# Two stacked transformer blocks on one core: the tile scheduler orders the instructions by a full timeline of the engines

## The chip, the cores and the metric

The kernel runs on one core of a Trainium2 chip. The metric is the device time of one execution in microseconds (us), the median over three runs. The engines are TensorE (PE, with PEld for its weight loads), VectorE (DVE), ScalarE (ACT), GpSimd (POOL) and SyncE (SP); each works through its own instructions strictly in the order in which they stand in its program, and waits on semaphores for the others.

## The reference

256 tokens of width 1024 go through two blocks of two layers each, all in float32:

```python
# first block, i = 0, 1
h = h + (ab_mixer if i == 0 else nsa_mixer)(rms_norm(h, g), ...)   # retention + mLSTM, or sparse attention
h = h + conv_ffn(rms_norm(h, ffn_norm_g[i]), ...)                  # 1024 -> 2 x 2816 -> 1024
e = rms_norm(p[i] @ ple_w[i], ple_norm_g[i])
h = h + sigmoid(rms_norm(h, ple_gate_norm_g[i]) @ ple_w_gate[i]) * e
# second block, l = 0, 1: hybrid layer
h = rms_norm_2(x, norm_g) * (1 + scale) + shift
a_qkv, a_z, m_cq, m_ckv, m_kr, m_z, merge = split(h @ w_in)
y_a = dilated_mixer(a_qkv, rel_bias) * silu(a_z)      # 24 heads in 3 groups, bias by distance, softmax
y_m = mla_mixer(m_cq, m_ckv, m_kr, ...) * silu(m_z)   # 16 heads, low-rank q and kv, causal softmax
merged = g_a * (y_a @ w_out_a) + g_m * (y_m @ w_out_b)
x = x + gate * (merged @ w_o)
# at the end rms_norm_2(x, final_norm_g)
```

## The kernel before

The 256 tokens are two blocks of 128 rows (tb0 and tb1). The activations stay in SBUF; what streams is weights, 253 MB of DMA, in tiles of 128 x 1024. Each weight tile takes three steps in `wt()`: SP issues the DMA into `raw` (L442, five buffers), ACT rounds it to `whi` (L448), and DVE subtracts to get the rest, `wlo` (L449); both have four buffers. PE then computes every product three times in float32r (`mm3`, L465 to L467):

```python
mm(out, lhsT=a[0], rhs=b[0], start=start, stop=False)
mm(out, lhsT=a[0], rhs=b[1], start=False, stop=False)
mm(out, lhsT=a[1], rhs=b[0], start=False, stop=stop)
```

Activations are split likewise after a transpose on PE (L577), into `xh` by ACT (L581) and `xl` by DVE (L582). Products gather in `acc` tiles, of which PSUM holds three.

The phases run one after the other: the AB mixer (0 to 130 us), FFN, PLE gate (341 to 372), the sparse attention NSA (372 to 530), FFN, PLE gate (723 to 753), the two hybrid layers (753 to 1110 and 1110 to 1480) and the last norm. Within a phase the program is written as one list of operations; the order on each engine is the choice of the tile scheduler, which takes the operations whose inputs and buffers it expects to be there.

In the AB mixer retention and mLSTM attend in pieces (scores L812, L813 and L828, DVE weights L816 and L818, outputs L820 to L822). Their heads are then squared on ACT (L855), reduced on DVE (L856), and an inverse root is found by integer and Newton steps on DVE (L591 to L595). `cat` (L873 for retention, L895 for mLSTM) takes that and the gates, and its transposes (L577) feed the output product. PLE computes one norm on POOL (L627 to L631, `half` L960), and its update of `h` (L966) needs it.

In a hybrid layer `quad` attends with four heads at a time. For each head a bias tile is fetched by a DMA on the ACT queue into one of two buffers; the scores come from PE (L1466), DVE adds the bias and finds the maximum (L1469), ACT takes the exponent (L1474), DVE normalises (L1475, L1476), PE transposes (L677), DVE and ACT copy (`pT`, L680, L682) and PE multiplies by v (`po`, L685, L688). `mla_chunk` does the same for the other attention (scores L1557, exponent L1562):

```python
bt = ph.tile([P, 1024], F32, tag="bias", bufs=2, name=self.nm("bias"))
nc.scalar.dma_start(bt, bass.AP(b0.tensor, ...))
nc.vector.tensor_tensor_reduce(p[:, g0:g1], s3, b3[:, g0:g1, T - nk:], -1.0, 3e38, ALU.add,
                               ALU.min, nm[:, j:j + 1])
```

Products of `w_in` that follow in the program are what the scheduler can put between the steps of these chains.

Of the kernel before, what the change touches and what calls it, by code (L numbers as in the profile page):

```python
# [16 lines left out]
T = 256  # L17
# [4 lines left out]
W = 1024  # L22


# ------------------------------------------------------------------ layout
# The weights are cut into tiles of at most 128 x 1024 in the order in which
# the kernel consumes them.  A tile is a list of pieces (array, index, rows,
# columns) laid side by side.
# [28 lines left out]
def plan():  # L57
# [6 lines left out]
    def nat(key, arr, ix, cols, nkb, row0=0):  # L64
        """tiles of row blocks x 512 columns"""
        per = W // len(cols)
        for t in range(0, nkb, per):
            add((key, t // per), [(arr, ix, row0 + kb * P, cols) for kb in range(t, min(nkb, t + per))])

    def tr(key, arr, ix, cols, nkb=8):  # L70
        """one tile per 128 columns, all row blocks"""
        add((key, 0), [(arr, ix, kb * P, cols) for kb in range(nkb)])

    # AB mixer
# [31 lines left out]
    # NSA mixer  # L106
# [15 lines left out]
    # hybrid layers  # L122
# [70 lines left out]
# per-feature vectors as columns of one [128, n] array  # L193
# [72 lines left out]
def pack_rows(inp):  # L266
    """vectors that are spread over all partitions by the load"""
    return np.concatenate([inp["ple_norm_g"][0], inp["ple_norm_g"][1], inp["final_norm_g_2"],
                           inp["b_ada_2"][0][2048:], inp["b_ada_2"][1][2048:], inp["c_2"][0]])[None, :]


def constants():
    """[128, n] tables that depend on shapes alone"""
# [4 lines left out]
    # rotary tables of the retention, [2 heads x 64, 256]  # L278
# [7 lines left out]
    # swap of the halves of each head  # L286
# [4 lines left out]
    # decay of the retention in [key, query]: 256 queries for key block 0, 128 for block 1  # L291
# [10 lines left out]
    # NSA: causal mask of the last key block, validity of the compressed keys  # L302
# [13 lines left out]
    # sum of four partial sums that lie below each other  # L316
    c["nsa.st4"] = (p[:, None] % 32 == np.arange(30)[None, :]).astype(f)
    c["nsa.blk"] = (p[:, None] // 16 == np.arange(8)[None, :]).astype(f)
    # rotary tables of the MLA, rows: even heads, odd heads, cos, sin; columns: frequency, quarter
    # turns, phase, amplitude  # L320
# [21 lines left out]
    # buckets of the relative positions, reversed: column m is the distance 255 - m  # L342
# [30 lines left out]
# ------------------------------------------------------------------ kernel  # L373
class Builder:
# [54 lines left out]
    # -- weights: load, split into two float32r parts  # L429
    def wt(self, key, dst=None):  # L430
        """dst: pairs of tiles for the two parts, one for each block of rows or one for all"""
# [4 lines left out]
        if dst is None:  # L436
            # in the FFN some go where the PLE keeps its weights
# [24 lines left out]
    def mm3(self, out, a, b, start, stop):  # L462
        """out += a^T b with a = (hi, lo), b = (hi, lo)"""
# [5 lines left out]
    def gates(self, key, n, xs):  # L469
        """x W for n columns: [128 tokens, 2, n] in PSUM"""  # L470
# [11 lines left out]
    def nat(self, key, xs, nkb, w=512, fill=False, last=0, sc=False):  # L482
        """x W for both blocks of 128 tokens: two [128, w] in PSUM.  last: the first block is done early"""
# [26 lines left out]
    def nat_tb(self, key, xs, dst, evac, early):  # L510
        """x W for 1024 columns: the first block of tokens is done before the second, by all products of that
        if early, else by those of the last 512 columns.
        dst(c, t): where the parts of the weights go, evac(columns, tb, acc)"""
# [30 lines left out]
    def tr(self, keys, xs, nkb=8, w=P):  # L544
        """(x W)^T for one or two blocks of columns: [w, 2, 256] in PSUM"""
# [7 lines left out]
    def tr_start(self, keys, xs):  # L553
        """as tr, blocks in banks of their own, the first half of the rows of all blocks before the second:
        it can begin when half of x is there"""
# [10 lines left out]
    def make_xT(self, src, nkb, gain=None, dst=None):  # L566
        """src(tb, kb): [128 tokens, 128 features].  Transposed, times gain, split."""
# [18 lines left out]
    # -- 1/sqrt of a small tile, by Newton steps from an estimate in the exponent  # L586
# [15 lines left out]
    def meansq(self, dst, src):  # L602
        """a column of the sums of src^2 / 2048"""
# [3 lines left out]
    def rstd(self, src, name):  # L607
        """1/rms of the rows of src [128, 2, 1024]: [128, 2]"""
# [12 lines left out]
    def norm_newton(self, n, tb, j=1, eng=None):  # L621
        """Newton steps from an estimate in the exponent, for one block of tokens; the sum is in columns 0 and j"""
# [3 lines left out]
        # x is half the mean; the sign of y turns with each of the three steps  # L626
# [6 lines left out]
    def norm_tb(self, tb):  # L633
        """the norm of h for one block of tokens, at the end of the part before the one that needs it"""
# [15 lines left out]
    def row_bc(self, col, name):  # L650
        """[128, 2] per token -> [128, 256], the same row in all partitions"""
# [15 lines left out]
    def pv_pair(self, po, p0, p1, v, ns, start):  # L667
        """po [2 heads x 64, 256 queries] += v^T p^T over ns sources.  p0(e, s): [128 queries, 128 keys] of
        the first query block, p1(e, s): [128, 256] of the second, v(s, kb, e): [128 keys, 64]"""
# [39 lines left out]
    # ---------------------------------------------------------------- AB mixer  # L709
    def ab(self):  # L710
# [9 lines left out]
        # input and forget gates, [token, 4 + 4]  # L720
# [4 lines left out]
        # q, k of the mLSTM: convolution over time, silu (times 2)  # L725
# [17 lines left out]
        # v with a column of ones  # L743
# [9 lines left out]
        # log sigmoid(x) = min(x, 0) - 2 atanh((1 - t) / (3 + t)), t = tanh(|x| / 2)  # L753
# [13 lines left out]
        # rows over the tokens: i, log f  # L767
# [21 lines left out]
        # q, k of the retention: rotary  # L789
# [60 lines left out]
        # norms over each head  # L850
# [26 lines left out]
        # den = max(|den|, exp(-m)); 0.5 / den * rsqrt(ss / (128 den^2) + eps)  # L877
# [22 lines left out]
    # ---------------------------------------------------------------- FFN  # L900
# [33 lines left out]
    # ---------------------------------------------------------------- PLE  # L934
    def ple(self, i):
# [5 lines left out]
        # e = rms(p W) g / 2  # L941
# [34 lines left out]
    # ---------------------------------------------------------------- NSA mixer  # L976
    def nsa(self):
# [9 lines left out]
        # keys and values of the two branches  # L987
        def head_factor(src, nh, out, scale):
            """r * rsqrt(r^2 ss / 64 + eps) * scale for each head of src(tb) [128, nh, 64]: out [128, 2, nh]"""
# [12 lines left out]
        # raw keys and values of the compression, [2 tokens x 64, group, 256]  # L1002
# [39 lines left out]
        # in the places of tensors that are not there yet  # L1042
# [5 lines left out]
        # gates  # L1048
# [11 lines left out]
        def compress(kv):  # L1060
            n = "kv"[kv]
            # four row blocks at once, side by side in the array
# [10 lines left out]
            # gelu, tanh form  # L1073
# [66 lines left out]
        def attention(g, qT):  # L1140
            # compressed branch, all heads of the group at once
# [66 lines left out]
    # ---------------------------------------------------------------- tables of the hybrid layers  # L1208
    def rope_tables(self):
        """[128, 4, 256]: q of the even heads, q of the odd heads, cos, sin"""  # L1210
# [34 lines left out]
    def bias_rows(self):  # L1245
        """biases by distance, invalid distances at -1e30, in DRAM: 23 copies of
        [8 heads, 3 groups, 384], so that the row of
        partition 16 a + b, 16 a + b places earlier, can be read from copy a + b with positive strides"""
# [23 lines left out]
    def side_work(self):  # L1272
        """work that waits for nothing, done beside products that leave VectorE idle"""
# [7 lines left out]
    def ada(self):  # L1281
        """shift and scale as columns [128, 16], the gate in all partitions [128, 1024]"""
# [9 lines left out]
        # silu(c) along the rows  # L1292
# [34 lines left out]
    # ---------------------------------------------------------------- hybrid layer  # L1327
# [390 lines left out]
```

## Time and profile before

| | before |
|---|---|
| median of three runs (lowest, highest) | 1482.52 us (1481.35, 1489.27) |
| span of the profiled execution | 1490.1 us |
| PE busy / PEld busy | 1431.5 us (96%) / 1220.8 us (82%) |
| DVE busy | 1034.1 us (69%) |
| ACT busy / POOL busy | 759.8 us (51%) / 26.4 us (2%) |
| chain that ended last | PE 81%, DVE 7%, DMA 5%, ACT 3%, issue 2%, POOL 2% |

The profiled execution is one run of its own. Its span, from the first to the last instruction, lies just above the slowest of the three timed runs, 0.5% above their median; nothing around the span is recorded for it. A busy PE in these rows is a PE with a matmul in its pipe; that it goes at full pace is only seen from the rate of matmuls and from the busy share of PEld.

### The profile page before, as it was taken

What the parts mean: (1) busy time and instruction counts of PE and PEld (TensorE: products, weight loads), DVE (VectorE), ACT (ScalarE), POOL (GpSimd) and SP (SyncE); (2) the same over time, 40 slices, a digit from 0 to 9 for tenths busy, and PEclk for the clock granted to TensorE, in tenths of its full rate; (3) what the DMA queues carried; (4) which work ended last, traced back from release to release, by engine and by line L of the source; (5) the groups of instructions that cost most, each with busy time, mean ns of one, the idle gap of its engine ahead of it and who ended that gap; (6) DMA issues with size and microseconds to landing.
All of it is one profiled execution on the core that took longest, in us unless ns stands there. A gap on an engine that the chain in (4) does not pass through costs nothing.

```text
span 1490.1 us, 23718 instructions
## 1 busy us (share of the span) xinstructions
PE 1431.5 (96%) x9011; PEld 1220.8 (82%) x9011; DVE 1034.1 (69%) x2250; ACT 759.8 (51%) x1383; POOL 26.4 (2%) x41
## 2 busy tenths in 40 slices
PE   8999979999999999999989999999999999999997
PEld 7878979988755699997787878879879797979886
DVE  7678758987777788897677744556577865456466
ACT  6355635536455665553557543434555753334443
POOL 0000000003000000000300000000000000000000
PEclk9999989999989999999999999989999999999999
DMA  7444556895630266687533444525553444443561
GB/s 264 140 146 156 177 174 232 307 322 193 235 128 1 70 214 213 213 297 280 192 127 93 147 151 128 177 70 191 188 197 129 125 147 130 142 151 117 191 200 61
DMA packets 72734, 253.99 MB, mean 170 GB/s; under 512 B 8187, under 2 KB 11795, under 8 KB 72469
## 3 DMA queue, kind: packets, MB, share of 16 engines
q1 hardware_dynamic: 68880, 239.87, 48.5%
q10 hardware_dynamic: 3740, 12.61, 2.9%
q8 instruction: 71, 1.16, 0.3%
q14 instruction: 43, 0.35, 0.1%
HBM read 251.36 MB, written 1.93 MB: 170 GB/s over the span
## 4 chain that ended last, share of the span: by engine, by line
PE 81%; DVE 7%; DMA 5%; ACT 3%; issue 2%; POOL 2%; SPq 0%; POOLq 0%; ACTq 0%; DVEq 0%
PE acc L465 21%; PE acc L467 21%; PE acc L466 21%; PE po L685 4%; PE tp L677 3%; DMA raw<-weights 3%; DVE wlo L449 2%; DMA bias<-brow 2%; PE sc L1178 2%; PE sc L1466 1%; ACT whi L448 1%; PE po L688 1%; POOL rs L631 1%; PE sc L1557 1%; DMA gb<-rows 1%
## 5 line engine op out<-in xcount | busy, mean ns | idle before, releaser
L449 DVE TENSOR_TENSOR wlo<-raw,whi 128x1024 fp32r<-128x1024 f32 (+2 forms) x386 | 460.6, 1197 | 216.8 <-ACT whi L448 213.2
L448 ACT ACTIVATE whi<-raw 128x1024 fp32r<-128x1024 f32 (+2 forms) x386 | 398.7, 1036 | 356.1 <-PE acc L467 184.6
L465 PE MATMUL acc<-xh,whi 128*128 128x256 f32 (+1 forms) x1360 | 390.1, 288 | 17.1 <-DVE zp L920 8.8
L466 PE MATMUL acc<-xl,whi 128*128 128x256 f32 (+1 forms) x1360 | 389.6, 287 | 0.7 <-DVE xl L582 0.7
L467 PE MATMUL acc<-xh,wlo 128*128 128x256 f32 (+1 forms) x1360 | 388.0, 286 | 0.5 <-DVE wlo L449 0.3
L465 PEld LDWEIGHTS acc<-xh,whi 128*128 128x128 f32 (+1 forms) x1360 | 261.0, 192 | 26.5 <-DVE zp L920 9.0
L466 PEld LDWEIGHTS acc<-xl,whi 128*128 128x128 f32 (+1 forms) x1360 | 261.4, 192 | 4.5 <-issue 2.5
L467 PEld LDWEIGHTS acc<-xh,wlo 128*128 128x128 f32 (+1 forms) x1360 | 261.2, 192 | 1.5 <-DVE wlo L449 0.9
L465 PE MATMUL acc<-whi,xh 128*128 128x512 f32 (+2 forms) x688 | 249.1, 363 | 2.3 <-DVE xh L1355 1.2
L467 PE MATMUL acc<-whi,xl 128*128 128x512 f32 (+2 forms) x688 | 248.9, 363 | 1.3 <-DVE xl L582 1.2
L466 PE MATMUL acc<-wlo,xh 128*128 128x512 f32 (+2 forms) x688 | 248.4, 361 | 0.0
L465 PEld LDWEIGHTS acc<-whi,xh 128*128 128x128 f32 x688 | 130.3, 189 | 24.0 <-ACT xh L581 2.2
L467 PEld LDWEIGHTS acc<-whi,xl 128*128 128x128 f32 x688 | 130.0, 189 | 22.2 <-DVE xl L582 2.5
L466 PEld LDWEIGHTS acc<-wlo,xh 128*128 128x128 f32 x688 | 130.3, 189 | 19.2 <-issue 1.7
L465 PE MATMUL acc<-whi,gh 128*128 128x512 f32 x176 | 70.1, 398 | 0.0
L467 PE MATMUL acc<-whi,gl 128*128 128x512 f32 x176 | 69.4, 394 | 0.0
L466 PE MATMUL acc<-wlo,gh 128*128 128x512 f32 x176 | 69.3, 394 | 0.0
L680 DVE COPY pT<-tp 128x384 f32<-128x384 f32 x56 | 31.2, 557 | 41.6 <-PE tp L677 41.4
L677 PE MATMUL tp<-const_g,pr 128*128 128x128 f32 x336 | 56.9, 299 | 0.7 <-DVE pr L1566 0.7
L677 PEld LDWEIGHTS tp<-const_g,pr 128*128 128x128 f32 x336 | 38.9, 149 | 19.4 <-issue 12.3
L682 ACT ACTIVATE pT<-tp 128x384 f32<-128x384 f32 x56 | 27.1, 485 | 45.8 <-PE tp L677 40.7
L1466 PE MATMUL sc<-qk,qk 64*128 64x256 f32 (+1 forms) x192 | 41.9, 379 | 8.6 <-DVE nmx L1469 8.1
(411 smaller groups left out, 1914.8 us busy)
## 6 DMA issues: line engine op xcount, KB each, us to landing
raw<-weights SPq DMA_DIRECT2D x384, 512.0 KB
adw<-weights SPq DMA_DIRECT2D x48, 512.0 KB
bias<-brow ACTq DMA_DIRECT2D x16, 512.0 KB
w<-weights SPq DMA_DIRECT2D x8, 512.0 KB
raw<-weights SPq DMA_DIRECT2D x8, 416.0 KB
const_ab<-consts SPq DMA_DIRECT2D x1, 1536.0 KB
h<-x SPq DMA_DIRECT2D x4, 256.0 KB
gb<-rows ACTq DMA_DIRECT2D x2, 512.0 KB
```

The lines of the kernel that those rows point to most:

```text
L448: nc.scalar.activation(hi, r, AF.Copy)
L449: nc.vector.tensor_tensor(lo, r, hi.bitcast(F32), op=ALU.subtract)
L465: mm(out, lhsT=a[0], rhs=b[0], start=start, stop=False)
L466: mm(out, lhsT=a[0], rhs=b[1], start=False, stop=False)
L467: mm(out, lhsT=a[1], rhs=b[0], start=False, stop=stop)
L631: ts(y[:, o], t[:, o], 1.5, y[:, o], ALU.subtract, ALU.mult)
L677: nc.tensor.transpose(tp[:, j * P:(j + 1) * P], a, self.ident)
L680: nc.vector.tensor_copy(pT, tp[:, :384])
L682: nc.scalar.activation(pT, tp[:, :384], AF.Copy)
L685: nc.tensor.matmul(po[e * 64:e * 64 + 64, :], lhsT=v(s, 0, e), rhs=pts[e][:, 0:T], start=start and s == 0, stop=False)
L1178: nc.tensor.matmul(s4, lhsT=qT[hs, pr, tb * P:(tb + 1) * P], rhs=kT[hs, g, :, 0:nk], start=True, stop=True)
L1466: nc.tensor.matmul(s3[:, g - g0], lhsT=qs[g][hs, pr, tb * P:(tb + 1) * P], rhs=ks[g][hs, pr, :nk], start=True, stop=True)
```

## The change

One argument of the tile context in `kernel()` is new. With it the scheduler still builds the order of each engine from the same operations, but decides which operation comes next by a timeline of all engines that it keeps while it goes, where its default goes by a simpler estimate. Comments were removed as well, without a change of the line numbers. No operation, tile, buffer count or queue is changed.

```diff
-    with tile.TileContext(nc) as tc:
+    with tile.TileContext(nc, schedule_with_timeline_sim=True) as tc:
         with ExitStack() as ctx:
             Builder(ctx, tc, aps).run()
```

The programs of the engines hold the same instructions before and after, but for one load of a function table less on ACT (the sine of L1238 now comes ahead of the first gelu of L926, where it stood between two). On PE 4426 of 8438 instructions stand elsewhere, by up to 186 places. POOL's order is the same, and SP's DMAs move by two places at most.

The first place is the quad attention of the first hybrid layer on PE (it begins at 875 us before). `acc_9462` is a product of `w_in` that nothing in the attention needs, the `sc` tiles are scores. Before:

```order
4752 L1466 MATMUL sc_9267<-qk_9008,qk_8945 128x256
4753 L1466 MATMUL sc_9271<-qk_9197,qk_9134 128x256
4754 L465 MATMUL acc_9462<-xh_7834,whi_9464 128x256
4755 L466 MATMUL acc_9462<-xl_7835,whi_9464 128x256
4756 L467 MATMUL acc_9462<-xh_7834,wlo_9465 128x256
4757 L465 MATMUL acc_9462<-xh_7834,whi_9464 128x256
4758 L1466 MATMUL sc_9279<-qk_8253,qk_8190 128x128
```

And the same scores of the change, with the last of the product's matmuls ahead of them:

```order
4776 L465 MATMUL acc_9462<-xh_7834,whi_9464 128x256
4777 L466 MATMUL acc_9462<-xl_7835,whi_9464 128x256
4778 L467 MATMUL acc_9462<-xh_7834,wlo_9465 128x256
4779 L1466 MATMUL sc_9279<-qk_8253,qk_8190 128x128
4780 L1466 MATMUL sc_9279<-qk_9008,qk_8945 128x128
4781 L1466 MATMUL sc_9279<-qk_9197,qk_9134 128x128
```

`sc_9271` stands at 4754 there: 24 matmuls of the product lie between it and `sc_9279`, where there were 4. Up to the scores `sc_9379` of the third head, whose bias tile is the first that has to wait for a buffer, there are 84 such matmuls in place of 24. The other three quads are changed alike.

The second place is DVE at the same scores (L1469 is the bias and maximum, L1476 the normalisation, L449 a weight split). Before:

```order
1447 L1469 ISA pr_9278,nmx_9264<-sc_9279,bias_9262 128x384
1448 L1469 ISA nmx_9264 128x1
1449 L1469 ISA pr_9291,nmx_9289<-sc_9292,bias_9287 128x512
1450 L1469 ISA nmx_9289 128x1
1451 L1475 RECIPROCAL l_9265<-l_9265 128x1
1452 L1469 ISA pr_9291,nmx_9289<-sc_9296,bias_9287 128x256
1453 L1469 ISA nmx_9289 128x1
1454 L1476 TENSOR_SCALAR pr_9266<-pr_9266,l_9265 128x768
```

And of the change:

```order
1428 L1476 TENSOR_SCALAR pr_9266<-pr_9266,l_9265 128x768
1429 L1469 ISA pr_9278,nmx_9264<-sc_9279,bias_9262 128x384
1430 L1469 ISA nmx_9264 128x1
1431 L449 TENSOR_TENSOR wlo_9591<-raw_9589,whi_9590 128x1024
1432 L1469 ISA pr_9291,nmx_9289<-sc_9292,bias_9287 128x512
1433 L1469 ISA nmx_9289 128x1
```

Four weight splits (`wlo_9591`, `wlo_9597`, `wlo_9654`, `wlo_9684`) now stand among the softmax steps of the first two biases, where there was none.

The third place is PE in the AB mixer, at the last pieces of retention (`tp_845` is an output, `acc_874` and `acc_875` a gate product). Before:

```order
372 L822 MATMUL tp_835<-vr,aw_833 128x128
373 L820 MATMUL tp_845<-vr,aw_843 128x128
374 L821 MATMUL tp_845<-vr,aw_843 128x128
375 L822 MATMUL tp_845<-vr,aw_843 128x128
376 L467 MATMUL acc_874<-whi_877,xl_100 128x512
377 L465 MATMUL acc_875<-whi_877,xh_99 128x512
```

And of the change, where `cat` is what the head norms produce:

```order
466 L813 MATMUL sc_840<-rqk 128x128
467 L820 MATMUL tp_845<-vr,aw_843 128x128
468 L821 MATMUL tp_845<-vr,aw_843 128x128
469 L822 MATMUL tp_845<-vr,aw_843 128x128
470 L577 MATMUL tp_1072<-const_g,cat 128x128
471 L577 MATMUL tp_1081<-const_g,cat 128x128
```

The 92 product matmuls that stood between the last L822 and the first transposes of `cat` now stand ahead of the retention pieces.

Elsewhere three things move. In both PLE gates DVE's weight splits go ahead by up to 21 places, and the second products of `ple_w` come 20 PE places later. At the end of the first hybrid layer and of the kernel the matmuls of the last three output tiles, which stood one tile after the other, are interleaved. The last DVE steps of tb0's final norm come to stand among those of tb1's.

## Rows read from the trace of the kernel before

**Rows 1.** The page: the span, the engines' busy shares, the clock, the weight splits.

```profile
span 1490.1 us, 23718 instructions
...
PE 1431.5 (96%) x9011; PEld 1220.8 (82%) x9011; DVE 1034.1 (69%) x2250; ACT 759.8 (51%) x1383; POOL 26.4 (2%) x41
...
PEclk9999989999989999999999999989999999999999
...
L449 DVE TENSOR_TENSOR wlo<-raw,whi 128x1024 fp32r<-128x1024 f32 (+2 forms) x386 | 460.6, 1197 | 216.8 <-ACT whi L448 213.2
```

**Rows 2.** Busy us by stretch: PE, PEld, DVE, ACT, POOL (count), clock, DMA share.

```profile
54.00:82.00 28.00, 27.40 (x142) 20.27 (x141) 15.13 (x31) 10.58 (x19) 0.00 (x0) 1.00 0.33 109
82.00:106.00 24.00, 23.36 (x105) 18.55 (x103) 20.96 (x52) 13.99 (x19) 0.00 (x0) 1.00 0.48 149
755.00:875.00 120.00, 116.36 (x846) 105.27 (x846) 81.37 (x225) 70.27 (x169) 0.00 (x0) 0.99 0.43 133
875.00:911.00 36.00, 33.63 (x191) 22.64 (x189) 19.32 (x54) 14.03 (x29) 0.00 (x0) 0.91 0.43 114
911.00:957.00 46.00, 46.00 (x383) 45.46 (x381) 19.52 (x18) 18.20 (x20) 0.00 (x0) 1.00 0.51 165
957.00:998.00 41.00, 39.29 (x224) 26.83 (x224) 22.19 (x58) 15.47 (x31) 0.00 (x0) 0.88 0.25 78
1155.00:1237.00 82.00, 79.79 (x598) 71.51 (x598) 57.23 (x164) 49.17 (x119) 0.00 (x0) 1.00 0.44 142
1237.00:1273.00 36.00, 33.87 (x193) 22.67 (x192) 19.33 (x54) 13.86 (x29) 0.00 (x0) 0.91 0.41 116
1318.00:1345.00 27.00, 24.62 (x143) 16.80 (x143) 16.54 (x50) 11.45 (x25) 0.00 (x0) 0.94 0.30 98
```

**Rows 3.** Chain that ended last, 868 to 900 us: start, us, what.

```profile
868.06 0.12 PE acc L467
...
879.12 0.48 ACT pr L1474
879.60 7.70 DMA bias<-brow
887.42 0.69 DVE pr L1469
```

**Rows 4.** Timeline of DVE in the AB mixer: start, us, line; idle before in brackets.

```profile
82.75 0.69 DVE L856 TENSOR_REDUCE ssr<-sqj 128x4 f32<-128x512 f32 x1 [2.37 <-ACT sqj L855]
...
87.15 0.17 DVE L595 SCALAR_TENSOR_TENSOR r<-rst,r 128x8 f32<-128x8 f32 x1
87.35 0.17 DVE L593 TENSOR_TENSOR rst<-r 128x8 f32<-128x8 f32 x1
...
90.04 0.36 DVE L863 TENSOR_SCALAR f<-r,half 128x4 f32<-128x4 f32 x2
...
95.02 1.28 DVE L873 TENSOR_TENSOR cat<-gt,f 128x512 f32<-128x512 f32 x2
...
104.77 1.28 DVE L895 TENSOR_TENSOR cat<-gt,f 128x512 f32<-128x512 f32 x2
```

**Rows 5.** Timelines of POOL and DVE in the first PLE gate.

```profile
352.79 4.78 POOL L631 TENSOR_SCALAR rs<-mt,rs 128x1 f32<-128x1 f32 x1
...
360.98 0.30 POOL L631 TENSOR_SCALAR rs<-mt,rs 128x1 f32<-128x1 f32 x1
...
352.78 4.63 DVE L449 TENSOR_TENSOR wlo<-raw,whi 128x1024 fp32r<-128x1024 f32 x4
...
363.31 0.75 DVE L966 SCALAR_TENSOR_TENSOR h<-gt,half,h 128x512 f32<-128x512 f32 x1 [3.61 <-POOL half L960]
```

**Rows 6.** Chain that ended last, from 1476 us to the end: start, us, what.

```profile
1475.83 0.23 PE acc L465
...
1484.22 0.28 DVE mt L630
...
1485.89 0.72 ACT o L1647
```

## The prediction

> **What bounds the kernel now.** I read the page first. PE is busy for 96% of the span, but PEld only for 82%, and the row of the clock has single slices below full speed [rows 1]. A share of 96% would leave 60 us to gain, if it were true. It is not the whole truth, so the next view is busy time by stretch [rows 2]. The reader should compare two kinds of stretch there. From 911 to 957 us PE has nothing but products: 383 matmuls in 46 us, PEld busy for 45.46 of 46, clock 1.00. That is the pace at which the kernel can go, one matmul in 0.12 us [rows 3]. From 875 to 911, the quad attention just ahead of it, PE is called busy for 33.63 of 36 us, but PEld only for 22.64, and the granted clock is 0.91 on average: part of the stretch runs at 1.2 GHz in place of 2.4. The other quads look the same, and the two MLA stretches look so in a milder form. So PE bounds the kernel, and what it loses lies in the attention stretches, where it works in the beat of a chain through DVE, ACT and a DMA. The chain of waits shows the heaviest link [rows 3]: the exponent of the second head at 879.12, behind it on ACT's queue the third bias, 7.70 us of DMA, and only at 887.42 the DVE step that reads it.
>
> The sum is made against the profiled execution, 1490.1 us, and carried to the median of the runs (1482.5) by their ratio, 0.995.
>
> **The change part by part.** Nothing is added or removed except one table load on ACT, so all cost and gain is in where PE stands still.
>
> *The four quads, a gain.* What is lost there in plain sight is idle time and clock; clock lost is length times (1 - clock). From [rows 2]: 875 to 911, 2.37 + 36 x 0.09 = 5.6; 957 to 998, 1.71 + 41 x 0.12 = 6.6; 1237 to 1273, 2.13 + 3.24 = 5.4; 1318 to 1345, 2.38 + 27 x 0.06 = 4.0. Together 21.6 us. Behind that lies a loss that PE's row doesn't show. Had PEld been as busy as in the product stretch (98.8%), it would have had 35.6 us instead of 22.6 in the first quad, and likewise 40.5, 35.6 and 26.7 in the others: 49.4 us of shortfall in all. That is an upper bound, because a matmul of the attention takes longer than its weight load. The new order puts 84 matmuls of products, not 24, ahead of the scores that stand behind the third bias. The 60 more are 60 x 0.12 = 7.2 us of work against a wait of about 2.3 us, so the wait is covered even if the chain itself becomes 2 or 3 us later by the products that stand in it (20 more of them ahead of the second scores, 2.4 us). Those products need four more weight splits during the softmax, 4 x 1.2 = 4.8 us on DVE [rows 1], which is busy for 19.32 of 36 there: the room exists, but the chain gets longer by part of it. I take 28 us for the four, above the plain loss because the whole stretch fills up, and far from the upper bound. Bounds: 9 (the idle time alone, no clock) to 45.
>
> *The MLA stretches, a gain.* 3.64 + 1.2 from 755 to 875 and 2.21 from 1155 to 1237 are 7.1 us [rows 2]; the products between the scores L1557 are fewer there than in the quads. I take 4, between 0 and 7.
>
> *The AB mixer, a loss.* Today 92 product matmuls, 21 us at 0.23 each [rows 6], run while DVE does the head norms; PE loses only 0.6 us from 54 to 82 and 0.64 from 82 to 106 [rows 2]. In the change these products run first, and the last retention output is followed by nothing but transposes of `cat`, which must wait for the norm. That wait can be laid out from [rows 4]: squares on ACT 2.37, reduction 0.69, scale and integer step 0.4, nine Newton operations at a distance of 0.2 (87.15 to 87.35) 1.8, factor 0.36, `cat` 1.28, and about 0.8 for the split after the transposes: 7.7 us. After waits of 2 us and more PE is granted half its clock for a while; the quads above lose 1.6 to 4.9 us by that, and I take 2.5. Of the 1.2 us that are lost today most come back. The term is +9. Low bound 3, if mLSTM pieces and spread waits leave part of the norm ahead of the last retention piece. High bound: the whole chain from 82.75 to 106.05 less nine splits of 1.14 that stand in it, 13.0, with 4 for the clock: 17.
>
> *The PLE gates.* The second `ple_w` products come 20 places later, 20 x 0.23 = 4.6 us, and POOL's norm starts from them, so `half`, for which DVE waits 3.61 us today, could be late by 4.6 in each gate. But POOL's own time isn't fixed: the same L631 takes 0.30 us at 360.98 and 4.78 at 352.79, exactly while DVE runs four splits back to back for 4.63 us [rows 5]. In the change these splits stand ahead of the norm. I take 0 for both gates together, since the two effects are of one size and the gate's products go on for 7 us behind `half` anyway; bounds -6 to +9.
>
> The Trainium skill says why POOL is slow there: "GPSIMD Engine Reference", Specifications and Key points, has GpSimd share its SBUF interfaces with VectorE and contend with DVE instructions that have two SBUF inputs, which a split has. The trace agrees (4.78 against 0.30 us). By that rule alone the gates would gain what the splits cost POOL, and the total would be some 6 us lower; by the rows with the late start alone, 9 higher.
>
> *Small places.* At the hand-over from the first hybrid layer to the second, three interleaved output tiles let tb0 end later, at most by the 19 matmuls of 0.23 of one tile, 4.4 us; its norm then has less cover. I take +2. In the tail DVE's Newton steps of tb0 come among those of tb1 (0.28 and about 0.2 each, three rounds [rows 6]): +2 on the path that ends the kernel, between 0 and 4. The FFN's first norm broadcast moves behind other work: +1. NSA keeps its few filler products, so 0, between -3 and +3. The table load less lies on ACT, which is busy for half of the time: 0.
>
> *Sum.* -28 - 4 + 9 + 0 + 2 + 2 + 1 = -18 against 1490.1, or 1472; against the median 1482.5 - 18 x 0.995 = 1464.6. I say **1465**.
>
> **The rivals.**
>
> *A, the forecast.* The quads give 18 to 32 and AB takes 5 to 13: 1452 to 1475.
>
> *B, the stalls only move.* DVE and ACT are strictly in order. A split that comes ahead of a softmax step delays the chain by 1.2 us each, and a score that stands behind 24 products is 2.9 us later, so the third bias is issued later too. If the attention thereby stretches to the end of the products and still finds PE without work, only the idle time of [rows 2] is gained: 8.6 in the quads and 2 in MLA, against +14 elsewhere. Net +3: 1486, no change within 0.5%, which is about what a measurement of this kernel can tell. For it: DVE is the largest releaser in these stretches. Against it: 7.2 us of products against a wait of 2.3.
>
> *C, slower, by the AB mixer.* If the norms of both halves of `cat` stand bare, PE stops for 13 us and loses clock after it, +17, and the same starvation (products drawn ahead, nothing left for the end) costs +6 in NSA, where PE has the least filler. With 4 to 5 of the small places and a gain of 12 in the attention this is 1482.5 + 16 = 1498. It decides from the point at which AB and NSA lose more than the hybrid layers gain. For it: the order shows not one product behind the last retention piece. Against it: AB happens once, the quads four times.
>
> *D, all of the attention.* If the quads come near the upper bound (45) and MLA gives its 7 while POOL in the gates is freed from the splits (6), with AB at +9: -49 + 5 = -44, 1439.
>
> **How the numbers follow.** A 0.60, B 0.18, C 0.12, D 0.10. The range leaves out half of D below and most of C above: 1442 to 1488. Faster than 1475.1 are A, nearly all of it, and D: 0.69. Within 0.5% is B and the edge of A: 0.19. Slower is C: 0.12.
>
> **What would show it.** In the changed profile the stretches that hold the quads should have a PEld share of 80% or more, clock 1.00 and no PE wait on L1469. Ahead of the transposes of `cat` (L577, near 105 us) PE should have one wait of 7 to 10 us on DVE, with half clock behind it. POOL's L631 should hold none of 4.78 us, or its chain should end as late as today. If the quads show the same PEld share over a longer stretch, B is right. The forecast is wrong if waits of several us stand in NSA, which I set to zero, or if PE waits for raw weights, since more products early ask for DMAs early.

## The result, and the profile after

| | before | after |
|---|---|---|
| median (lowest, highest), four runs each | 1483.44 us (1481.35, 1489.27) | 1525.58 us (1522.97, 1529.91) |
| span of the profiled execution | 1490.1 us | 1524.5 us |

The ratio is 1.028 (95% interval 1.024 to 1.032): the kernel is 42 us slower. The prediction was 1465 us, faster, with a range up to 1488. Its sign and its range were wrong.

The page of the changed kernel, the lines that answer to [rows 1]:

```profile
span 1524.5 us, 23740 instructions
...
PE 1436.6 (94%) x9011; PEld 1230.0 (81%) x9011; DVE 1039.8 (68%) x2250; ACT 759.3 (50%) x1382; POOL 22.6 (1%) x41
...
PEclk9989989999986999999999999999999999999999
```

The work is the same (9011 matmuls, DVE and ACT within 6 us), and PE stands idle for 1524.5 - 1436.6 = 87.9 us where it was 58.6. So 29 of the 34 us between the two spans are PE waiting, and the 5 us more of busy time go with a lower clock (0.970 in the mean, where it was 0.976). The row of the clock says where to look: one of its 40 slices of 38 us is down at 6 (the thirteenth, from 457 us, in NSA), and from there to the end all are 9, where before the slice of one quad fell to 8.

The busy us by stretch say it in numbers (columns as in [rows 2]). The lines are the AB mixer's norm, a part of NSA, the first two quads, the hand-over between the hybrid layers, and the last two quads:

```profile
101.00:113.00 12.00, 3.63 (x17) 2.70 (x16) 9.77 (x32) 5.56 (x10) 0.00 (x0) 0.69 0.11 39
440.00:476.00 36.00, 27.77 (x90) 17.56 (x89) 26.71 (x115) 17.70 (x47) 0.00 (x0) 0.59 0.23 74
910.00:1038.00 128.00, 128.00 (x926) 109.35 (x925) 73.95 (x144) 56.48 (x90) 0.00 (x0) 1.00 0.46 140
1152.00:1162.00 10.00, 5.72 (x35) 5.10 (x34) 9.41 (x24) 5.38 (x17) 0.00 (x0) 0.91 0.66 229
1272.00:1407.00 135.00, 135.00 (x983) 115.74 (x981) 76.34 (x146) 59.13 (x93) 0.00 (x0) 1.00 0.46 141
```

The same two pairs of quads before, with the products between them:

```profile
876.00:1016.00 140.00, 135.92 (x937) 112.10 (x936) 73.55 (x144) 56.45 (x91) 0.00 (x0) 0.94 0.42 129
1232.00:1375.00 143.00, 138.49 (x982) 116.23 (x981) 75.55 (x146) 58.64 (x93) 0.00 (x0) 0.96 0.43 133
```

The quads do what was forecast. PE is without a gap, PEld is at 85%, the clock is 1.00, and the two pairs with what lies between them are some 12 and 8 us shorter (the first window holds 11 matmuls fewer, 1.3 us at 0.12). What was lost lies elsewhere: a hole of 8 us in 12 in the AB mixer, 36 us of NSA at a mean clock of 0.59 with PE idle for 8, and a hole of 4 us at the hand-over between the hybrid layers.

PE's waits over the whole changed kernel, the largest (us in total, times, the longest):

```profile
PE acc L465 <- DVE cy L927: 12.5, 3, 9.5
PE acc L465 <- ACT whi L448: 8.9, 6, 2.7
PE tp L577 <- DVE cat L873: 8.4, 1, 8.4
PE acc L465 <- DVE zp L921: 7.6, 2, 4.6
PE acc L465 <- DVE xh L1355: 7.3, 3, 3.7
PE tp L1132 <- DVE qn L1127: 5.4, 1, 5.4
```

No wait on L1469 is left. The wait for `cat` is the one that the prediction had laid out. The waits for `zp` (the first rows of an FFN that need its norm), `xh` of L1355 (the starts of the hybrid layers, 3.7 of it at the hand-over) and `qn` (NSA) stand at places that it had set to +1, +2 and 0. The waits for `whi` are new: before, PE had none. Half of them, 4.2 us, stand between the norm and the first quad of the second hybrid layer, and the longer one ends with ACT's rounding of a tile whose raw weights came late, which the prediction had named as a sign of being wrong:

```profile
1206.94 1.06 ACT L448 ACTIVATE whi<-raw 128x1024 fp32r<-128x1024 f32 x1 [2.76 <-DMA raw<-weights]
```

The largest, for `cy`, is hardly a new loss: it is the place in the first FFN where weights land late, while a DMA of 37 us that writes the table of biases is under way, and before PE stood still there for 12.0 us too (8.8 and 3.2).

### The profile page after: what moved, and what is told of

It reads as the page before. It is cut to its first block, busy times and chain, and to the rows that moved or that the text cites. A ratio compares the mean times of both kernels' runs of the same rounds, so it can differ in the third digit from the quotient of the medians.

```text
span 1524.5 us, 23740 instructions
## 1 busy us (share of the span) xinstructions
PE 1436.6 (94%) x9011; PEld 1230.0 (81%) x9011; DVE 1039.8 (68%) x2250; ACT 759.3 (50%) x1382; POOL 22.6 (1%) x41
## 4 chain that ended last, share of the span: by engine, by line
PE 83%; DMA 6%; DVE 6%; ACT 3%; issue 2%; SPq 0%; ACTq 0%; DVEq 0%
PE acc L465 22%; PE acc L467 21%; PE acc L466 21%; PE po L685 4%; PE tp L677 3%; DMA raw<-weights 3%; PE sc L1466 2%; DMA brow<-brow 2%; DVE wlo L449 1%; PE sc L1178 1%; ACT whi L448 1%; PE sc L1557 1%; PE po L688 1%; PE tp L577 1%; PE sc L465 1%
## 5 line engine op out<-in xcount | busy, mean ns | idle before, releaser
L449 DVE TENSOR_TENSOR wlo<-raw,whi 128x1024 fp32r<-128x1024 f32 (+2 forms) x386 | 460.3, 1197 | 235.8 <-ACT whi L448 232.0
L465 PE MATMUL acc<-whi,xh 128*128 128x512 f32 (+2 forms) x688 | 252.6, 369 | 14.9 <-DVE xh L1355 7.3
L1307 DVE CUSTOM_DVE_ANT_0 adw<-adw,ada 128x1024 f32<-128x1024 f32 x32 | 39.1, 1222 | 18.9 <-DMA adw<-weights 18.5
```

What stands on the lines that cost most here:

```text
L449: nc.vector.tensor_tensor(lo, r, hi.bitcast(F32), op=ALU.subtract)
L1307: nc.vector.tensor_tensor_reduce(raw, raw, cr, 1.0, 0.0, ALU.mult, ALU.add, m[:, j:j + 1])
```

## The experiments

All kernels do the same operations. To set an engine's order apart from the scheduler's choice they use one tool: a table of instructions, of which each is tied to the one ahead of it on its engine. (`nums` is the table, `traced` finds an instruction by its number.) The tie is on issue order alone; it adds no wait. With all engines in the table, a stretch that stands in the order before repeats it: f2 below reaches its first changed stretch at 875.6 us, the kernel before at 875.7.

```diff
+def pin(tc, table):
...
+    last = {}
+    for n in nums:
+        i = traced.get(n)
+        if i is None:
+            continue
+        p = last.get(i.engine)
+        if p is not None:
+            tc.add_manual_dep(i, p.name, mybir.DependencyInfo(mybir.DependencyClass.NoSync,
+                                                              mybir.DependencyReason.DATA), reason="pin")
+        last[i.engine] = i
```

Every ratio below is against runs of the kernel before on the same chip (medians of 1485 to 1487 us).

### Which engine's order

Theory S said that DVE and ACT are at fault, whose weight splits now stand ahead of chain steps; theory P that PE is, whose products are drawn ahead. Two kernels take the changed scheduler and tie PE, or DVE and ACT, to the order before; two take the scheduler of before and tie PE, or DVE and ACT, to the changed order. The engines without a tie are ordered by the scheduler that is named.

```diff
-    with tile.TileContext(nc) as tc:
+    with tile.TileContext(nc, schedule_with_timeline_sim=True) as tc:
         with ExitStack() as ctx:
             Builder(ctx, tc, aps).run()
+            pin(tc, ORDER)
```

This is the edit of e1 (ORDER is PE's order before) and e2 (DVE's and ACT's order before). In e3 (PE's changed order) and e4 (DVE's and ACT's changed order) only the last line is added.

> The full timeline still orders DVE, ACT and SP, but PE's 8438 instructions are pinned to the order of the kernel before. Theory S (the loss comes from weight splits that the timeline puts ahead of chain steps on DVE and ACT): slower than before by the FFN start, NSA and MLA, some 20 to 30 us, 1505 to 1515 us, and no gain in the quads. Theory P (the loss comes from PE's order, products drawn ahead of chains that then stand bare): within 0.5% of before, about 1483 us.

> The full timeline orders PE, but DVE and ACT are pinned to the order of the kernel before. Theory S: most of the loss goes, 1475 to 1495 us, with the quads still faster. Theory P: near the changed kernel, about 1515 to 1525 us.

> The default estimate orders DVE, ACT and SP, but PE is pinned to the order of the changed kernel. Theory S: the bare chain in the AB mixer (+12) and the interleaved tiles at the hand-over (+12) against the gain in the quads (-18), about 1485 to 1495 us. Theory P: about 1525 us, as the changed kernel.

> The default estimate orders PE, but DVE and ACT are pinned to the order of the changed kernel, with its splits ahead. Theory S: slower than before, 1505 to 1520 us. Theory P: within 0.5% of before.

| | median us | ratio (95% interval) |
|---|---|---|
| e1: PE as before, rest by the timeline | 1537.65 | 1.035 (1.031 to 1.039) |
| e2: DVE and ACT as before, PE by the timeline | 1585.64 | 1.067 (1.064 to 1.069) |
| e3: PE as changed, rest by the default | 1528.6 | 1.029 (1.027 to 1.031) |
| e4: DVE and ACT as changed, PE by the default | 1546.32 | 1.041 (1.038 to 1.043) |

Neither theory holds. Of the four forecasts of S none came in, and of those of P only that for e3 (about 1525). PE back in its old order should have given 1483 by P and stayed as slow as the change (1.035 against 1.028); DVE and ACT back should have given 1475 to 1495 by S and gave the slowest kernel of all. One engine tied to one plan, with the others ordered anew around it, was never better than the change whole: e3 equals it, e2 and e4 are clearly worse. So the four say little about the whole. By place they say something. PE's longest wait around the AB mixer's norm in e3:

```profile
PE tp L577 <- DVE cat L873: 8.0, 1, 8.0
```

In e1 `cat` is no longer waited for, and the longest wait there is 1.3. That wait comes and goes with PE's order. The gain of the quads goes with it too: they are as short in e3 as after the change, and no shorter than before in e1.

### Place by place

Theory L took the change as a sum of places, each with its own gain or loss. To test it, all engines stand in the order before, except over one place, where all engines stand in the changed order. Only places at which both orders have issued the same set ahead can be cut out so.

```diff
     with tile.TileContext(nc) as tc:
         with ExitStack() as ctx:
             Builder(ctx, tc, aps).run()
+            pin(tc, ORDER)
```

> All engines in the changed order through the AB mixer (to the end of its output product), all in the order before from there. Theory L (each place costs by itself, and the places add up): the step that the changed trace shows there, +12 us, so about 1495 us. Theory M (the orders only cost because a stage starts late or with other buffers than it was laid out for, so that a stage alone costs nothing): 1483 us.

> All engines in the order before, except the two stretches from the first quad score of a hybrid layer to the end of its second quad, which stand in the changed order. Theory L: the quads' steps in the changed trace, about -6 and -8, with the products drawn ahead of them some more: 1463 to 1473 us. Theory M: no gain, 1483 us or slower.

> All engines in the order before, except NSA and the start of the second FFN, which stand in the changed order. Theory L: the step of that stretch in the changed trace, +13 and +4, so 1497 to 1503 us. Theory M: about 1483 us.

> The order before on all engines, except the start of the first hybrid layer and its MLA (up to the first quad score), which stand in the changed order. If places add up as the AB, quad and NSA runs showed: the changed trace lost 5.5 us from the end of the second PLE gate to the first quad score, so about 1491 us against 1486. My prediction's own step for MLA, a gain of 2 us a layer: 1484 us.

> The order before on all engines, except the hand-over from the first hybrid layer to the second (its three output tiles, the norm and the first products of the second layer), which stands in the changed order. If places add up: +8.7 and +2.3 as in the changed trace, about 1497 us. My prediction's own term, +2: 1488 us.

> Only the start of the second FFN stands in the changed order, on all engines. The changed trace lost 4.2 us there behind three weight splits on DVE ahead of the step that frees PE's accumulators, and the run with NSA lost 4.5: +4 us, 0.3%, at the edge of what three rounds show.

| place in the changed order | median us | ratio (95% interval) | us | predicted |
|---|---|---|---|---|
| f1: start to end of the AB mixer | 1500.24 | 1.010 (1.007 to 1.014) | +15 | +9 |
| f4: NSA and the start of the FFN behind it | 1503.67 | 1.012 (1.006 to 1.018) | +18 | 0 |
| h4: the start of that FFN alone | 1488.59 | 1.002 (0.998 to 1.005) | +3, not told from 0 | 0 |
| g2: hand-over between the hybrid layers | 1500.14 | 1.010 (1.006 to 1.013) | +14 | +2 |
| g1: start of the first hybrid layer, its MLA (half of the forecast -4) | 1492.46 | 1.003 (1.000 to 1.005) | +4 | -2 |
| f2: the four quads | 1473.0 | 0.991 (0.989 to 0.994) | -13 | -28 |

The us are ratio less one, times the 1486 of before. The five places that don't overlap (without h4) add up to +38, of the +42 of the change. The intervals of the five, taken as independent, leave some 13 us either way on that sum, and the gates, the first FFN, the MLA of the second layer and the tail were not run alone. Four of the five are clear of no change, against theory M, and g1 is at its edge; all came within some 5 us of what was expected of them by theory L. So L holds: the places cost by themselves, and they account for the change as far as can be told.

In f1, PE's wait for `cat` is that of the changed kernel, 8.4 us.

In f4, NSA with the start of the FFN:

```profile
375.00:563.00 188.00, 172.12 (x912) 120.39 (x911) 134.65 (x477) 94.60 (x246) 0.00 (x0) 0.90 0.33 112
```

and the same work before:

```profile
375.00:547.00 172.00, 167.79 (x921) 116.11 (x921) 132.59 (x479) 95.78 (x248) 0.09 (x1) 0.94 0.35 120
```

It takes 16 us longer: 11.7 of them are more idle time (15.9 instead of 4.2), 4.3 more busy time at a lower clock. The longest wait is that for `qn`, the normed queries. Before, DVE's two batches of it (one for each block of rows) are 15 us apart, with PE's last 20 or so products and the scores of the first batch between them:

```profile
423.19 1.29 DVE L1127 TENSOR_TENSOR qn<-qn,qf 128x512 f32<-128x512 f32 x2
438.50 1.29 DVE L1127 TENSOR_TENSOR qn<-qn,qf 128x512 f32<-128x512 f32 x2
```

After the change both come late and together, behind four weight splits among the steps of the norm (the last is shown), and PE has run all its products ahead of the first:

```profile
446.85 1.22 DVE L449 TENSOR_TENSOR wlo<-raw,whi 128x1024 fp32r<-128x1024 f32 x1
...
449.44 1.29 DVE L1127 TENSOR_TENSOR qn<-qn,qf 128x512 f32<-128x512 f32 x2
451.90 1.29 DVE L1127 TENSOR_TENSOR qn<-qn,qf 128x512 f32<-128x512 f32 x2
```

In f2 the quads are the same stretch as after the change, within a microsecond (the second window holds 8 matmuls fewer than that of the change above):

```profile
876.00:1004.00 128.00, 128.00 (x928) 109.26 (x926) 73.72 (x144) 56.29 (x90) 0.00 (x0) 1.00 0.46 140
1221.00:1355.00 134.00, 134.00 (x975) 115.23 (x975) 76.33 (x146) 58.75 (x92) 0.00 (x0) 1.00 0.47 142
```

### Are the splits the cause?

In the changed order DVE and ACT issue weight splits just ahead of the chain step that PE waits for. DVE's timeline of the changed kernel at the start of the first FFN (start us, us, line; idle before in brackets) shows three of them, and a step of the rotary table, ahead of `zp`, for which PE waits 4.6 us:

```profile
157.52 1.23 DVE L449 TENSOR_TENSOR wlo<-raw,whi 128x1024 fp32r<-128x1024 f32 x1 [0.93 <-ACT whi L448]
...
158.92 1.22 DVE L449 TENSOR_TENSOR wlo<-raw,whi 128x1024 fp32r<-128x1024 f32 x1
160.06 0.69 DVE L1237 TENSOR_SCALAR ang<-ang 128x1024 f32<-128x1024 f32 x1
160.66 1.22 DVE L449 TENSOR_TENSOR wlo<-raw,whi 128x1024 fp32r<-128x1024 f32 x1
161.79 0.75 DVE L921 TENSOR_TENSOR zp<-acc,rb 128x256 f32<-128x256 f32 x2
```

f3 keeps the changed kernel and puts such splits behind the chain step at five places (both FFN starts, NSA, the start of the first hybrid layer, the hand-over); PE is untouched.

DVE's order there, from the changed kernel to f3:

```diff
 L1231 TENSOR_SCALAR turns_1530<-turns_1530 128x256
 L1233 SCALAR_TENSOR_TENSOR ang<-turns_1530,ang 128x256 x3
+L921 TENSOR_TENSOR zp_1471<-acc_1347,rb_1343 128x256
+L921 TENSOR_TENSOR zp_1482<-acc_1349,rb_1343 128x256
 L449 TENSOR_TENSOR wlo_1625<-raw_1623,whi_1624 128x1024
 L1236 TENSOR_SCALAR ang<-ang,const_rp 128x256
...
 L1237 TENSOR_SCALAR ang<-ang 128x1024
 L449 TENSOR_TENSOR wlo_1697<-raw_1695,whi_1696 128x1024
-L921 TENSOR_TENSOR zp_1471<-acc_1347,rb_1343 128x256
-L921 TENSOR_TENSOR zp_1482<-acc_1349,rb_1343 128x256
```

> The changed order, with PE untouched; only at five places of DVE and ACT (starts of both FFNs, query norm of NSA, starts of both hybrid layers) the weight splits that stand ahead of a chain step are put behind it, 24 splits on DVE, 8 copies and three moved steps on ACT. Theory S in its narrow form (a split queued ahead of a chain step holds it up in an in-order queue): 4.6 + 3 + 5 + 3 + 3 us and the half clock behind some of these, so 1500 to 1510 us. Rival (the chains are late for other reasons, the splits only fill the wait): 1520 to 1526 us.

Measured: 1531.59 us, ratio 1.032 (1.025 to 1.038), not faster than the changed kernel, and above the range of the rival too. The narrow form of S falls. PE's waits of f3 show why. At the first FFN start, `zp` is down from 4.6 to 0.7.

A little later in that FFN, from 190 to 235 us, the longest wait for `cy` grows from 9.5 to 14.5. What ends it is a weight tile: ACT rounds it as soon as its DMA has landed, in f3 at 217.51 us and in the changed kernel at 218.14, the same moment within 0.7 us. What was won ahead of it is given back. PE's wait in f3, then ACT's step in f3 and in the changed kernel:

```profile
PE acc L465 <- DVE cy L927: 17.0, 2, 14.5
```

```profile
217.51 1.06 ACT L448 ACTIVATE whi<-raw 128x1024 fp32r<-128x1024 f32 x1 [11.62 <-DMA raw<-weights]
```

```profile
218.14 1.06 ACT L448 ACTIVATE whi<-raw 128x1024 fp32r<-128x1024 f32 x1 [11.63 <-DMA raw<-weights]
```

In NSA, from 436 to 460 us, `qn` falls from 5.4 to 3.8, and a step behind it that cost 1.6 now costs 5.4. The four splits stand behind the first batch of `qn` now, and ahead of the second and of `cmpu`:

```profile
PE sc L1085 <- DVE cmpu L1081: 5.4, 1, 5.4
PE tp L1132 <- DVE qn L1127: 3.8, 1, 3.8
```

```profile
447.21 4.62 DVE L449 TENSOR_TENSOR wlo<-raw,whi 128x1024 fp32r<-128x1024 f32 x4
```

At the start of the first hybrid layer a wait of 2.1 (`wv`) is new and none went; at the hand-over `xh` falls from 3.7 to 1.8, and a wait of 3.0 (`dg`) is new. What follows is that a split moved back from one step is missed or in the way at another: the splits have to be done somewhere in a place where PE has little other work. That was read from the waits. No run took the splits out of a place altogether, so f3 speaks against the narrow form of S only.

### The hand-over and NSA, engine by engine

These three split a place by engine.

```diff
             Builder(ctx, tc, aps).run()
+            pin(tc, ORDER)
```

ORDER is that of before everywhere but at the place; there it is, in g4, the changed order of PE alone, in h1 PE's changed order with DVE and ACT as the default estimate puts them, and in h2 PE's order before with DVE and ACT as the full timeline puts them.

> As the run on the hand-over, but only PE takes the changed order there (the three output tiles interleaved); DVE, ACT, SP and POOL keep the order before. If the interleaving costs the hand-over: the same as that run, about 1497 us. If the weight splits do that DVE and ACT run ahead of the norm's steps: 1486 to 1489 us.

> In NSA PE takes the changed order; DVE and ACT are ordered there anew by the default estimate; everything else stands in the order before. If PE's order makes the loss (products run ahead, nothing left beside the query norm): +10 us or more against before. If the splits that DVE and ACT run ahead make it: within 4 us of before.

> In NSA PE keeps the order before; DVE and ACT are ordered there by the full timeline; everything else stands in the order before. If the order of DVE and ACT makes the loss: +10 us or more. If PE's does: within 4 us of before. With both kernels slow, either order alone is enough to lose.

| | median us | ratio (95% interval) |
|---|---|---|
| g4 | 1491.45 | 1.003 (1.000 to 1.006) |
| h1 | 1504.25 | 1.013 (1.007 to 1.019) |
| h2 | 1499.22 | 1.007 (1.004 to 1.011) |

At the hand-over PE's interleaving, which the prediction had priced, is worth some 4 us of the 14 and by itself can't be told from no change; 1491 lies between the two forecasts for g4. The rest goes with the orders of DVE and ACT, by subtraction: no run took these alone there. PE has two holes in g2. The first, 3.4 us, is a wait for `xh`, the split of the last product's input, the longest here:

```profile
PE acc L465 <- ACT xh L581: 4.1, 2, 3.4
```

On ACT two roundings of weights stand ahead of that `xh`, and the first waits for its DMA; before, `xh` stood between the two.

```profile
1101.87 0.90 ACT L448 ACTIVATE whi<-raw 128x832 fp32r<-128x832 f32 x1 [3.30 <-DMA raw<-weights]
...
1103.72 0.64 ACT L581 ACTIVATE xh<-tp 128x256 fp32r<-128x256 f32 x2
```

The second is in the norm. The chain that ended last in g2:

```profile
1130.00 1.65 ACT wv L448 x5
...
1132.09 1.28 DVE xt L1348 x4
1133.37 1.34 DVE wv L449 x4
1134.71 0.34 DVE xh L1355
```

Splits of `wv` stand on ACT, ahead of the norm's `xt` on DVE, and again between `xt` and `xh`. PE's wait there:

```profile
PE acc L465 <- DVE xh L1355: 3.7, 1, 3.7
```

Before, PE's longest wait from 1095 to 1150 us was 0.5. In the changed kernel the second hole is the same (3.7), and the first is spread over three waits of 0.7 to 1.3.

In NSA both kernels lose, and the place of the wait is the same. PE's waits in h1, and then in h2:

```profile
PE tp L1132 <- DVE qn L1127: 5.6, 1, 5.6
```

```profile
PE tp L1132 <- DVE qn L1127: 5.8, 2, 3.9
```

Before, the same wait was 1.3:

```profile
PE tp L1132 <- DVE qn L1127: 1.3, 1, 1.3
```

These two don't set PE's order apart from the splits cleanly. In h1 the default estimate, given PE's changed order, puts four splits ahead of `qn` as well (426.10 to 432.20 us), so the loss there is PE's order with the splits that follow from it. And both tie one engine and order others anew around it, which by itself went with a loss in e1, e2 and e4.

### The better version

g3 takes the changed order for the four quads and the second PLE gate, and the order before everywhere else, by the edit of the places above.

> The order before, with the four quads in the changed order as in the run that gained 13 us, and with the second PLE gate in the changed order too, where the changed trace gained 4.6 us. If places add up: 1468 to 1470 us against 1486; if the gain of the gate was only the cover that the late stages before it left, 1473 us.

Measured: 1470.76 us, ratio 0.990 (0.987 to 0.993), 15 us faster than the kernel before and 55 less than the change. Nearly all of it is the quads: f2 alone gave 0.991 (0.989 to 0.994), and g3 can't be told from that. The second gate takes 36.6 us in g3, from the last update of `h` by the FFN (L707) to that by the gate (L966), where it took 38.0 to 39.3 in the runs that have it in the order before; that is about 2 us, not the 4.6 expected. The first line of its page:

```profile
span 1470.7 us, 23719 instructions
```

## Why the prediction was wrong, step by step

**The step that failed** is the one that set places to nothing: "NSA keeps its few filler products, so 0, between -3 and +3". With the start of the FFN behind it, it cost 18 us (f4), and the hand-over, at +2, cost 14 (g2). With -28 and +9 as forecast, these two alone would have turned -18 into +12. The reasoning looked at how much work PE has beside the chain, and not at what stands ahead of the chain's steps on DVE and ACT, nor at how PE's filler is spread over the chain. The chain steps there were all in the trace, and [rows 2] has no row of NSA at all: the stretch was never laid out. What the runs showed in its place: in NSA both batches of `qn` come behind four weight splits and after all of PE's products, with a wait of 5.4 us and half clock behind it; at the hand-over roundings and splits of weights stand ahead of `xh`, with waits of 3.4 and 3.7 us. From -18 to +42 are 60 us: NSA is 18 of them, the quads 15, the hand-over 12, the AB mixer 6, the start and MLA of the first layer 6. Rival C had the mechanism (work drawn ahead, starvation in AB and NSA) and the sign, at a chance of 0.12 and with +6 for NSA; 1498 was still 28 us short.

**The quads** were right in mechanism, wrong in size: -13 in the runs (interval -10 to -16) and -18.5 between the profiled executions of before and f2 (1490.1 and 1471.6 us), for a term of -28. Two causes. The stretch is full (PE 128 of 128 us, clock 1.00) with PEld at 85%, so the order has no more to gain there; the 21.6 us of visible loss alone would have been within 3 us of the trace. What I added for PEld's shortfall was the attention matmuls' own length and could not be gained. And the profiled execution of before had bad luck in just these quads. From the first score of a layer's first quad to that of its second, the same 564 matmuls took 81.2 and 81.0 us there, with the clock at 0.96; in five other executions in the old order they took 79.4 in the mean, and 77.2 to 77.9 where the clock stayed at 1.00. A term that is read from one execution carries its luck.

**MLA**, -4 for both layers, did not gain. g1, with the start and the MLA of the first layer, is at +4. That start had no term, and 12 matmuls have moved into it, so the two are read together, from the last transpose of the norm to the first quad score. In the second layer, before and then after:

```profile
1133.80:1237.50 103.70, 101.45 (x762) 92.58 (x761) 71.39 (x195) 60.02 (x139) 0.00 (x0) 1.00 0.41 134
```

```profile
1168.90:1278.70 109.80, 104.03 (x766) 94.38 (x764) 72.82 (x195) 60.38 (x139) 0.00 (x0) 0.98 0.40 125
```

PE is idle for 5.8 us where it was 2.2, and 4.2 of that are the two waits for `whi` shown above. In the first layer the same stretch takes 108.5 us instead of 105.7.

**The AB mixer** was right in mechanism and low in size. The one wait for `cat` was laid out as 7.7 us and is 8.4. The end of DVE's timeline there answers to [rows 4]:

```profile
104.60 0.69 DVE L856 TENSOR_REDUCE ssr<-sqj 128x4 f32<-128x512 f32 x1 [0.70 <-ACT sqj L855]
...
109.11 1.28 DVE L873 TENSOR_TENSOR cat<-gt,f 128x512 f32<-128x512 f32 x2
```

The links are those of the sum. The clock behind the wait was put at 2.5:

```profile
110.10:115.70 5.60, 5.60 (x17) 4.25 (x17) 5.24 (x23) 2.86 (x6) 0.00 (x0) 0.50 0.00 0
```

PE is busy there throughout at half clock, so it cost 2.8. These 11.2 us are most of the 15 (with 5 either way) of the run; what else PE waited for at this place in f1 is three waits of 0.6 to 0.9.

**The PLE gates**, 0, between -6 and +9, came out a little better: from the last update of `h` by the FFN (L707) to that by the gate (L966) they take 31.5 and 36.4 us in the trace of after, where it was 33.0 and 38.7. The reason is not the one that was weighed. POOL's norm, from its first step to `half`, is shorter by 2.8 and 1.0 us only (10.8 and 12.6 instead of 13.6 and 13.7). The 4.78 of [rows 5] is gone from L631, but splits still stand beside the norm, in shorter blocks, and other steps wait for them. POOL and DVE in the second gate after the change:

```profile
768.73 2.63 POOL L630 TENSOR_SCALAR mt<-rs,ms 128x1 f32<-128x1 f32 x1
```

```profile
768.88 2.35 DVE L449 TENSOR_TENSOR wlo<-raw,whi 128x1024 fp32r<-128x1024 f32 x2
```

The rule cited from the Trainium skill, "GPSIMD Engine Reference", Specifications and Key points, is that GpSimd contends with DVE instructions of two SBUF inputs. These rows agree with it: a POOL step that takes 0.34 us elsewhere ends here with the block of splits. The 6 us that the rule alone gave did not come. Counted from the FFN's last update, `half` is 2.4 us later in the first gate and 0.2 earlier in the second, so what shortened the gates is not POOL's norm, and no run says what it is.

**The tail**, +2, is right within 1 us: from the first score of the last quad to the end it is 169.4 us in the trace of after and 168.3 in that of f2, which has the quad changed and the tail not. **The FFN's first norm**, +1, was more by the trace: the wait for `zp` at the first FFN is 4.6 us, where PE had none for it. It was not run alone.

**What stays open.** Which DVE and ACT steps cost h2 its 11 us isn't settled, nor why the raw weights come late for the second layer's MLA; nor whether the splits or PE's order weigh more in NSA. The start of the second FFN alone is below what the runs can tell. Orders of one engine from one plan with the other engines' from the other were tried whole and in part, but not at the AB mixer or the hand-over with DVE and ACT alone.

## What to carry to other kernels

A scheduler's other order is not one change but as many as there are stages: lay out each stage's chain, those that seem untouched too, by what stands ahead of each step on every in-order engine and by what filler PE has left behind it. Ask of every zero in the sum which row it rests on. An order can be taken stage by stage, at points where both have issued the same set. Take all engines of a stage together: orders mixed by engine over the whole kernel came out at 1.029 to 1.067 here.

## What the runs showed of the hardware

From the first score of a layer's first quad to that of its second, the changed order takes 76.3 or 76.4 us, in both layers and in each of the traces of after, f2, g3 and e3, with no wait on PE and the clock at 1.00. The order before took between 77.2 and 82.6 over six executions (before, f1, f4, g1, g2 and g4), for the same 564 matmuls, so at its best it was within 1 us. The waits differ little, 1.3 to 2.5 us; it is the clock that makes the spread. The two layers of one execution, g1, show it:

```profile
880.30:957.80 77.50, 75.79 (x565) 65.89 (x564) 38.69 (x72) 31.73 (x48) 0.00 (x0) 1.00 0.49 150
1240.10:1322.20 82.10, 80.38 (x565) 67.79 (x564) 38.75 (x72) 31.73 (x48) 0.00 (x0) 0.94 0.47 142
```

PE is idle for 1.7 us in each, 1.6 of it in one wait for L1469. In one layer the clock stayed at its upper level of 2.4 GHz, in the other it fell to 1.2 for a while and cost 4.6 us. Over the six executions four stretches kept 1.00 and took 77.2 to 77.9; two fell to 0.94 and took 82.1 and 82.6. The prediction's reading, half clock after waits of 2 us and more, is too simple for these rows: in h1, whose quads stand in the order before, a wait of 2.2 us in the second layer was followed by no drop (78.1 us), and in g2 one of 1.2 was followed by a drop (0.98, 78.6 us). What decides it no run shows. What the rows do show is that an order without the wait took the spread away as well as the mean.

And the lost clock can outweigh a wait. From 440 to 476 us of the changed kernel PE is idle for 8.2 us; it is busy for 27.77 at a mean clock of 0.59, of which 27.77 x 0.41 = 11.4 us are lost, by an estimate that takes all of the busy time as bound by the clock.
